# A hybrid decoder layer in float32: another order for the first loads, a shorter run-up and a shared first cast

## The chip, the cores and the metric

The kernel runs on one core of a Trainium2 chip. The metric is the device time of one execution in microseconds. A core has TensorE (PE in the profile, its weight loads PEld), VectorE (DVE), ScalarE (ACT), GpSimd (POOL) and SyncE (SP); DMAs are issued here by SyncE and ScalarE, each on a queue of its own.

## The reference, cut to what matters

One decoder layer over a sequence of 256 tokens with 2048 channels, all in float32. The change touches only the way into the first projection:

```python
h = rmsnorm(x, norm_mix_w[l])                       # x: (1, 256, 2048)
proj = jnp.einsum('bsd,de->bse', h, w_in[l])        # 2048 -> 14368 columns
q, k, v, z, b_raw, a_raw, p_in, g_a, g_b = jnp.split(proj, splits, axis=-1)
...                                                 # gated delta rule, pooling mixer, gates
x = x + jnp.einsum('bsd,de->bse', mixed, w_out[l])
...                                                 # norm, up projection, convolution, GELU
x = x + jnp.einsum('bsf,fd->bsd', jax.nn.gelu(gate, approximate=False) * up, w_down[l])
return rmsnorm(x, norm_final_w)
```

The per-token scale of the norm commutes with the product, so the kernel multiplies x only by the norm's channel weights before the projection and applies the scale later.

## The kernel before

Every large product is done in two parts per operand. A float32 tile is split into an upper part (a cast to fp32r, on ScalarE) and the rest (a subtraction on VectorE), and three products are added in PSUM: upper x times upper weight, lower x times upper weight, upper x times lower weight. Weights come as a list `srcs` of tiles of 256 rows by 512 columns (512 KB each). `load(n)` issues DMAs on SyncE until n tiles have been asked for, into four buffers `raw`; the first two tiles (`HALVES`) go as two DMAs of 256 KB each. `begin(n)` splits tiles into `whi` (L144, ScalarE) and `wlo` (L152, VectorE); for the first two tiles `begin_half(n, k)` does one half of 128 rows (L133, L134).

The start is written out by hand, and PE, DVE and ACT run it in the order of the program:

- `ones` and `ident` are made on GpSimd, and `runup(9)` lets TensorE multiply `ones` by `ones` nine times (L243). Each of these float32 products is two matmul records in the trace.
- ScalarE's queue loads `nmrows`, the norm's channel weights as 16 rows (L255). ScalarE then does one small copy, `first` (L258), ahead of which its function table is loaded.
- SyncE's queue loads x in four blocks of 512 columns, `x0[0]` to `x0[3]` (L263), with the weight tiles in between. The first block goes as two DMAs of 256 columns. The order is: x first half, weight tile 0 (two DMAs), x second half, weight tile 1 (two DMAs), x block 1, tiles 2 and 3, x blocks 2 and 3.
- TensorE transposes `nmrows` (L321) and VectorE copies the result to `nmw`, one weight for each partition and block of 128 channels.
- `turn_x` transposes x (L281), `parts_x` makes from each transposed block the upper part `xhi` on ScalarE (L287) and the lower part `xlo` on VectorE (L288), both scaled by `nmw`, and `products_k0` runs the products (L313): four with `whi`, then two with `wlo`, for each 128 channels.
- In the first round of the loop over halves there are no products yet; `runup(4)` is there in their place.

Then three blocks of x follow in the same way, and after them the rest of the layer, with weights loaded, split and multiplied in a steady order.

Of the kernel before, what the change touches and what calls it, by code (L numbers as in the profile page):

```python
# [7 lines left out]
F32 = mybir.dt.float32  # L8
# [5 lines left out]
P = 128  # L14
# [20 lines left out]
def kernel(  # L35
# [20 lines left out]
    nc = tc.nc  # L56
# [11 lines left out]
    def nm(s):  # L68
        cnt[0] += 1
        return f"{s}_{cnt[0]}"  # L70

    def pg(shape=(P, 512)):
        return psg.tile(list(shape), F32, tag="g", name=nm("psg"))
# [35 lines left out]
    loads = []  # L109
# [4 lines left out]
    def weights(ahead=AHEAD):  # L114

        begin(taken[0] + ahead + 1)
        taken[0] += 1
        return made[taken[0] - 1]

    def load(n):  # L120
        while len(loads) < min(len(srcs), n):
            src = srcs[len(loads)]
            raw = wpool.tile(list(src.shape), F32, tag="raw", name=nm("raw"), bufs=4)
            for k in range(2) if len(loads) < HALVES else (slice(None),):
                last_load[0] = nc.sync.dma_start(raw[:, k], src[:, k]).ins
            loads.append(raw)

    def begin_half(n, k):

        if k == 0:  # L130
            made.append(tuple(wpool.tile([P, 2, 512], F32R, tag=tag, name=nm(tag)) for tag in ("whi", "wlo")))
        hi, lo = made[n]
        nc.scalar.copy(hi[:, k], loads[n][:, k])  # L133
        nc.vector.tensor_tensor(lo[:, k], loads[n][:, k], hi[:, k].bitcast(F32), op=ALU.subtract)  # L134

    def begin(n):
        while len(made) < min(len(srcs), n):
            load(len(made) + 1)
            raw = loads[len(made)]
            shape = list(raw.shape)  # L140
            keep = kept.get(len(made))
            hi = wpool.tile(shape, F32R, tag="whi", name=nm("whi")) if keep is None else \
                mtile(keep, shape, F32R, nm("khi"))
            nc.scalar.copy(hi, raw)  # L144
            if shape[1] == 8:
                lo = None
                nc.vector.tensor_tensor(hi[:, :, 32:64], raw[:, :, 0:32], hi[:, :, 0:32].bitcast(F32),
                                        op=ALU.subtract)
            else:
                lo = wpool.tile(shape, F32R, tag="wlo", name=nm("wlo")) if keep is None else \  # L150
                    mtile(4 + keep, shape, F32R, nm("klo"))
                last_split[0] = nc.vector.tensor_tensor(lo, raw, hi.bitcast(F32), op=ALU.subtract).ins  # L152
            made.append((hi, lo))
# [87 lines left out]
    def runup(n):  # L241
        for _ in range(n):
            mm(pr0[:, 0, :P], ones, ones, start=True, stop=True)  # L243


    runup(9)

    def mtile(i, shape, dt, name):
        return big.tile(shape, dt, tag=f"m{i}", name=name)

    mix = tc.tile_pool(name="mix", bufs=1)
    mp = mix.__enter__()

    nmrows = mp.tile([KD, P], F32, tag="w1", name="nmrows")
    rows = nc.scalar.dma_start(nmrows, norm_mix_w[0].rearrange("(r p) -> r p", p=P))  # L255
    first = cpool.tile([P, 1], F32, name="first")
    with tc.issue_after(rows.ins):
        nc.scalar.copy(first, ones[:, 0:1])  # L258
    x0 = []
    for c in range(4):  # L260
        xc = mtile(c, [P, 2, 512], F32, f"x0_{c}")
        for h in ((0, 256), (256, 512)) if c == 0 else ((0, 512),):
            nc.sync.dma_start(xc[:, :, h[0] : h[1]], x[0, :, c * 512 + h[0] : c * 512 + h[1]]  # L263
                              .rearrange("(t p) d -> p t d", p=P))
            if h[0] == 0:
                load(min(c + 1, 4))
        x0.append(xc)
        load(min(2 * c + 2, 4))


    nmw = cpool.tile([P, KD], F32, name="nmw")
# [3 lines left out]
    def turn_x(c, ks=range(4)):  # L275

        pts = []
        for k in (4 * c + k for k in ks):
            pt = pg([P, S])
            for t in range(2):  # L280
                nc.tensor.transpose(pt[:, t * P : (t + 1) * P], x0[c][:, t, (k % 4) * P : (k % 4 + 1) * P], ident)  # L281
            pts.append((k, pt))
        return pts

    def parts_x(pts):
        for k, pt in pts:
            hi = nc.scalar.activation(xhi[:, k, :], pt, AF.Copy, scale=nmw[:, k : k + 1])  # L287
            lo = nc.vector.scalar_tensor_tensor(xlo[:, k, :], pt, nmw[:, k : k + 1], xhi[:, k, :].bitcast(F32),  # L288
                                                op0=ALU.mult, op1=ALU.subtract)
        return hi.ins, lo.ins  # L290
# [3 lines left out]
    def square_x(c):  # L294
        for t in range(2):
            junk = cpool.tile([P, 512], F32, tag="sqj", name=nm("junk"))
            nc.scalar.activation(junk, x0[c][:, t, :], AF.Square, accum_out=ssq4[:, t, c : c + 1])
# [10 lines left out]
    def products_k0(c, kks, hi, lo):  # L308
        for w, part in ((hi, xh), (hi, xl), (lo, xh)):
            for kk in kks:  # L310
                k = 2 * c + kk
                for t in range(2):
                    mm(ps_k0[:, t, :], part(k, t), w[:, kk, :], start=(k == 0 and w is hi and part is xh),  # L313
                       stop=(k == KD - 1 and w is lo))

    def tile_k0(c):
        products_k0(c, range(2), *weights(-1))

    with tc.manual_schedule(engines={mybir.EngineType.PE, mybir.EngineType.DVE, mybir.EngineType.Activation}):
        pt = pg()  # L320
        nc.tensor.transpose(pt[:, :KD], nmrows, ident[:KD, :KD])  # L321
        nc.vector.tensor_copy(nmw, pt[:, :KD])

        n = 0
        for c in range(HALVES):
            for k in range(2):
                if k == 0:
                    pts = turn_x(0, (2 * c, 2 * c + 1))
                parts_x(pts[k : k + 1])
                begin_half(c, k)  # L330
                if n == 0:
                    runup(4)
                else:
                    products_k0((n - 1) // 2, ((n - 1) % 2,), *made[(n - 1) // 2])
                n += 1
        taken[0] = HALVES
        for c in range(4):
            if c:
                tile_k0(2 * c)
            if c < 3:  # L340
                pts = turn_x(c + 1)
                parts_x(pts[:2])
                begin(2 * c + 3)
                last_act, last_dve = parts_x(pts[2:])
                begin(2 * c + 4)
                square_x(c)
            if c:
                tile_k0(2 * c + 1)
            else:
                products_k0(1, (1,), *made[1])  # L350
        square_x(3)
# [110 lines left out]
    for c in range(2):  # L462
        hi, lo = weights()
        for kk in range(8):
            k = 8 * c + kk
# [556 lines left out]
    for c in range(4):  # L1022
# [9 lines left out]
        for k2 in range(2):  # L1032
            pt = pg([P, 2, S])
            for kk in range(2):
                k = 4 * c + 2 * k2 + kk
                for t in range(2):
                    nc.tensor.transpose(pt[:, kk, t * P : (t + 1) * P], xt[:, t, k * P : (k + 1) * P], ident)
            for kk in range(2):
                k = 4 * c + 2 * k2 + kk
# [76 lines left out]
    for t in range(2):  # L1116
# [31 lines left out]
        n = len(blocks) - 1  # L1148
# [39 lines left out]
```

## Time and profile before

| | us |
|---|---|
| median of three runs | 1562.16 (1561.58 to 1562.27) |
| the profiled execution, its own time | 1561.54 |
| its span, first to last instruction | 1559.8 |
| TensorE busy | 1551.1 (99%) |
| VectorE busy | 1092.2 (70%) |
| ScalarE busy | 749.2 (48%) |
| DMA, mean over the span | 195 GB/s |

The profile is one execution of the program. A line in the timeline gives the start and the duration in microseconds, the engine, the line of the kernel, the operation and what it writes and reads. The names are those of the program without buffer numbers: `xhl` is the tile that holds `xhi` and `xlo`, `x` is `x0`. An `SPq` or `ACTq` line is the issue of a DMA, not the transfer; the DMA view gives the time from issue to landing.

### The profile page before, as it was taken

Reading aid. Unit: us, or ns where it says so; the run is one execution under the profiler, and the core shown is the slowest. Engines: PE = TensorE matmul, PEld = TensorE weight load, DVE = VectorE, ACT = ScalarE, POOL = GpSimd, SP = SyncE. Lnnn points to the kernel's source line nnn. Section 1 sums busy time; section 2 is a strip of 40 time slices with the busy share of each in tenths; the row PEclk is TensorE's granted clock in tenths of the full one; section 3 lists DMA queues with packets and bytes.
Section 4 is the critical chain, followed back from the end, with each engine's and each line's share of the span. In section 5 each row is a group of like instructions: output and inputs, shape, how many; then the busy total and the mean of one; then the engine's idle time right before and its main releaser. Section 6 shows DMA issues by size and latency. Waiting matters only on the chain.

```text
span 1559.8 us, 21250 instructions
## 1 busy us (share of the span) xinstructions
PE 1551.1 (99%) x7996; PEld 1304.0 (84%) x7996; DVE 1092.2 (70%) x1705; ACT 749.2 (48%) x969; POOL 52.2 (3%) x54
## 2 busy tenths in 40 slices
PE   9999999999999999999999999999999999999998
PEld 8878888888888888888888888888888888888886
DVE  6899758996699858896656666776666667444445
ACT  6545445454555445454544544444444444334443
POOL 1020001000010001000000000000000000000000
PEclk9999999999999999999999999999999999999999
DMA  8677657676676656675666666666666666666662
GB/s 273 201 239 200 186 161 223 204 204 183 174 218 202 194 174 191 211 205 174 216 188 176 190 188 189 189 190 188 189 183 195 188 187 212 196 192 210 200 222 93
DMA packets 168229, 304.21 MB, mean 195 GB/s; under 512 B 19235, under 2 KB 22835, under 8 KB 167999
## 3 DMA queue, kind: packets, MB, share of 16 engines
q1 hardware_dynamic: 165104, 297.84, 64.5%
q10 hardware_dynamic: 3022, 5.03, 1.0%
q8 instruction: 62, 1.02, 0.3%
q14 instruction: 41, 0.33, 0.1%
HBM read 297.56 MB, written 5.27 MB: 194 GB/s over the span
## 4 chain that ended last, share of the span: by engine, by line
PE 99%; issue 1%; ACT 0%; DVE 0%; POOL 0%; POOLq 0%
PE psm L182 15%; PE psm L184 15%; PE psm L183 15%; PE psm L206 11%; PE psg L206 10%; PE psg L1094 8%; PE psm L1094 7%; PE psg L207 5%; PE psm L207 5%; PE psm L313 1%; PE psg L672 1%; PE psg L227 1%; PE psg L674 0%; PE psm L243 0%; PE psg L809 0%
## 5 line engine op out<-in xcount | busy, mean ns | idle before, releaser
L152 DVE TENSOR_TENSOR wlo<-raw,whi 128x1024 fp32r<-128x1024 f32 x522 | 636.8, 1222 | 376.6 <-ACT whi L144 372.0
L144 ACT CAST whi<-raw 128x1024 fp32r<-128x1024 f32 x524 | 551.3, 1053 | 699.5 <-PE psm L183 293.8
L184 PE MATMUL psm<-wlo,xhl 128*128 128x512 f32 x864 | 339.1, 393 | 0.0
L183 PE MATMUL psm<-whi,xhl 128*128 128x512 f32 x864 | 339.0, 392 | 0.0
L182 PE MATMUL psm<-whi,xhl 128*128 128x512 f32 x864 | 339.0, 392 | 0.0
L206 PE MATMUL psm<-fhl,whi 128*128 128x512 f32 x704 | 246.2, 396 | 0.0
L206 PE MATMUL psg<-fhl,whi 128*128 128x512 f32 x704 | 238.0, 394 | 0.0
L207 PE MATMUL psm<-fhl,wlo 128*128 128x256 f32 x704 | 194.4, 279 | 0.0
L182 PEld LDWEIGHTS psm<-whi,xhl 128*128 128x128 f32 x864 | 162.3, 188 | 33.0
L183 PEld LDWEIGHTS psm<-whi,xhl 128*128 128x128 f32 x864 | 162.3, 188 | 32.9
L184 PEld LDWEIGHTS psm<-wlo,xhl 128*128 128x128 f32 x864 | 162.2, 188 | 32.7
L207 PE MATMUL psg<-fhl,wlo 128*128 128x256 f32 x704 | 178.7, 279 | 0.0
L206 PEld LDWEIGHTS psm<-fhl,whi 128*128 128x128 f32 x704 | 131.4, 188 | 30.5
L206 PEld LDWEIGHTS psg<-fhl,whi 128*128 128x128 f32 x704 | 129.2, 188 | 24.1
L207 PEld LDWEIGHTS psg<-fhl,wlo 128*128 128x128 f32 x704 | 132.5, 188 | 6.9
L207 PEld LDWEIGHTS psm<-fhl,wlo 128*128 128x128 f32 x704 | 132.6, 188 | 1.1
L1094 PE MATMUL psg<-whi,hhi 128*128 128x512 f32 (+1 forms) x170 | 66.0, 389 | 0.0
L1094 PE MATMUL psg<-whi,hlo 128*128 128x512 f32 (+1 forms) x170 | 65.9, 388 | 0.0
L1094 PE MATMUL psm<-whi,hlo 128*128 128x512 f32 x168 | 65.1, 388 | 0.0
L1094 PE MATMUL psm<-wlo,hhi 128*128 128x512 f32 x168 | 65.1, 388 | 0.0
L1094 PE MATMUL psm<-whi,hhi 128*128 128x512 f32 x168 | 65.1, 388 | 0.0
L1094 PE MATMUL psg<-wlo,hhi 128*128 128x512 f32 (+1 forms) x170 | 59.6, 388 | 0.0
(280 smaller groups left out, 1533.9 us busy)
## 6 DMA issues: line engine op xcount, KB each, us to landing
raw<-in_w_in_dram SPq DMA_DIRECT2D x224, 512.0 KB, 4.3
raw<-in_w_up_dram SPq DMA_DIRECT2D x176, 512.0 KB, 4.4
raw<-in_w_down_dram SPq DMA_DIRECT2D x88, 512.0 KB, 4.3
raw<-in_w_out_dram SPq DMA_DIRECT2D x32, 512.0 KB, 3.8
mv<-vrow SPq DMA_DIRECT2D x12, 512.0 KB, 5.7
taps<-in_conv_qkv_w_dram SPq DMA_DIRECT2D x16, 256.0 KB, 6.0
raw<-in_pool_w_dram SPq DMA_DIRECT2D x8, 512.0 KB, 3.7
vrow<-ev SPq DMA_DIRECT2D x4, 512.0 KB, 4.1
```

The costliest lines, as they stand in the source:

```text
L144: nc.scalar.copy(hi, raw)
L152: last_split[0] = nc.vector.tensor_tensor(lo, raw, hi.bitcast(F32), op=ALU.subtract).ins
L182: mm(ps[:, t, :], lh(k, t), hi[:, kk, :], start=(k == 0), stop=False)
L183: mm(ps[:, t, :], ll(k, t), hi[:, kk, :], start=False, stop=False)
L184: mm(ps[:, t, :], lh(k, t), lo[:, kk, :], start=False, stop=(k == nk - 1))
L206: mm(ps[f], hi[:, kk, fs], rhl(k), start=(k == 0), stop=False, skip_group_check=True)
L207: mm(ps[f][:, 1, :], lo[:, kk, fs], rhl(k)[:, 0, :], start=False, stop=(k == nk - 1), skip_group_check=True)
L227: nc.tensor.transpose(pt[:, ff, t * P : (t + 1) * P], src[:, t, f * P : (f + 1) * P], ident)
L313: mm(ps_k0[:, t, :], part(k, t), w[:, kk, :], start=(k == 0 and w is hi and part is xh), stop=(k == KD - 1 and w is lo))
L672: mm(pg0, kq[:, h, 0, 0:P], kq[:, h, :, :], start=True, stop=True)
L1094: mm(ps[:, cs], part(k, t), w[:, kk, cs], start=(k == first and n == 0), stop=(k == KF - 1 and n == 2), skip_group_check=last_block)
```

## The change

- `x0` is allocated ahead of the loads, and a helper `load_x(queue, c, h)` issues a part of it.
- The first half of the first x block is issued on ScalarE's queue, ahead of `nmrows`. SyncE's queue begins with weight tile 0; the order of the rest is as it was.
- `runup(9)` becomes `runup(7)`, and `runup(4)` in the first round is dropped.
- In `begin_half`, the very first half tile (n = 0, k = 0) is cast by two engines: columns 0 to 255 by ScalarE, columns 256 to 511 by VectorE. The other halves are cast by ScalarE alone.

```diff
     def begin_half(n, k):
...
-        nc.scalar.copy(hi[:, k], loads[n][:, k])
+        if n or k:
+            nc.scalar.copy(hi[:, k], loads[n][:, k])
+        else:
+            nc.scalar.copy(hi[:, k, :256], loads[n][:, k, :256])
+            nc.vector.tensor_copy(hi[:, k, 256:], loads[n][:, k, 256:])
         nc.vector.tensor_tensor(lo[:, k], loads[n][:, k], hi[:, k].bitcast(F32), op=ALU.subtract)
...
-    runup(9)
+    runup(7)
...
+    x0 = [mtile(c, [P, 2, 512], F32, f"x0_{c}") for c in range(4)]
+
+    def load_x(queue, c, h):
+        queue.dma_start(x0[c][:, :, h[0] : h[1]], x[0, :, c * 512 + h[0] : c * 512 + h[1]]
+                        .rearrange("(t p) d -> p t d", p=P))
+
+    load_x(nc.scalar, 0, (0, 256))
     nmrows = mp.tile([KD, P], F32, tag="w1", name="nmrows")
     rows = nc.scalar.dma_start(nmrows, norm_mix_w[0].rearrange("(r p) -> r p", p=P))
     first = cpool.tile([P, 1], F32, name="first")
     with tc.issue_after(rows.ins):
         nc.scalar.copy(first, ones[:, 0:1])
-    x0 = []
-    for c in range(4):
-        xc = mtile(c, [P, 2, 512], F32, f"x0_{c}")
-        for h in ((0, 256), (256, 512)) if c == 0 else ((0, 512),):
-            nc.sync.dma_start(xc[:, :, h[0] : h[1]], x[0, :, c * 512 + h[0] : c * 512 + h[1]]
-                              .rearrange("(t p) d -> p t d", p=P))
-            if h[0] == 0:
-                load(min(c + 1, 4))
-        x0.append(xc)
-        load(min(2 * c + 2, 4))
+    for n, c, h in ((1, 0, (256, 512)), (2, 1, (0, 512)), (4, 2, (0, 512)), (4, 3, (0, 512))):
+        load(n)
+        load_x(nc.sync, c, h)
...
                 begin_half(c, k)
-                if n == 0:
-                    runup(4)
-                else:
+                if n:
                     products_k0((n - 1) // 2, ((n - 1) % 2,), *made[(n - 1) // 2])
                 n += 1
```

## The prediction

> **What bounds the kernel now.** I read the head of the page first, then the waits of TensorE, then the stretch in which the program starts.
>
> ```profile
> span 1559.8 us, 21250 instructions
> PE 1551.1 (99%) x7996; PEld 1304.0 (84%) x7996; DVE 1092.2 (70%) x1705; ACT 749.2 (48%) x969; POOL 52.2 (3%) x54
> PE 99%; issue 1%; ACT 0%; DVE 0%; POOL 0%; POOLq 0%
> PE psm L243 <- POOL ones L233: 1.1, 1, 1.1
> 6.86:20.00 13.14, 13.14 (x68) 10.90 (x68) 9.86 (x16) 10.44 (x22) 0.00 (x0) 1.00 1.04 378
> ```
>
> The chain that ended last is TensorE for 99% of the span, and the only wait that the waits view lists for TensorE in the whole run is the 1.1 us for the first memset. The last row (a window; the columns are its length, the busy time and count of PE, PEld, DVE, ACT, POOL, then the granted clock, the DMA share and GB/s) says that this holds in the first microseconds as well: from 6.86 us on, TensorE has no idle time. So what comes before the first product is a constant in front of 1553 us of TensorE work, and whatever moves that product moves the end by as much, as long as nothing behind it starts to wait. The change touches only what lies before that product, and the instructions of all engines behind it stand in the same order as before.
>
> The start itself, from the timeline (start us, duration us, engine, line):
>
> ```profile
> 0.80 0.45 ACTq L255 DMA_DIRECT2D nmrows<-in_norm_mix_w_dram  x1
> 0.81 0.43 SPq L263 DMA_DIRECT2D x<-in_x_dram  x1
> 1.06 4.21 PE L243 MATMUL psm<-ones 128*128 128x128 f32 x18 [1.06 <-POOL ones L233]
> 1.28 0.93 SPq L125 DMA_DIRECT2D raw<-in_w_in_dram  x2
> 1.29 1.28 ACT L258 ACT_TABLE_LOAD   x1 [1.29 <-PEq L1172]
> 2.59 0.19 ACT L258 COPY first<-ones 128x1 f32<-128x1 f32 x1
> 5.20 0.23 PE L321 MATMUL psg<-ident,nmrows 16*128 16x16 f32 x1
> 5.36 0.66 PE L281 MATMUL psg<-ident,x 128*128 128x128 f32 x4
> 5.83 0.47 ACT L287 ACTIVATE xhl<-psg,nmw 128x256 fp32r<-128x256 f32 x1 [3.05 <-PE psg L281]
> 5.85 1.06 PE L243 MATMUL psm<-ones 128*128 128x128 f32 x8
> 6.21 0.61 ACT L133 CAST whi<-raw 128x512 fp32r<-128x512 f32 x1
> 6.34 0.48 DVE L288 SCALAR_TENSOR_TENSOR xhl<-psg,nmw,xhl 128x256 fp32r<-128x256 f32 x1 [0.70 <-ACT xhl L287]
> 6.71 0.48 ACT L287 ACTIVATE xhl<-psg,nmw 128x256 fp32r<-128x256 f32 x1
> 6.85 0.69 DVE L134 TENSOR_TENSOR wlo<-raw,whi 128x512 fp32r<-128x512 f32 x1
> 6.87 1.20 PE L313 MATMUL psm<-whi,xhl 128*128 128x512 f32 x4
> ```
>
> Nine run-up products are 18 passes and hold TensorE until 5.20. The norm row's transpose (L321) and those of x follow, ScalarE makes the upper part of x at 5.83, is free for its next instruction 0.38 later, casts the weights from 6.21 to 6.82, and the first product starts 0.05 later, at 6.87. The transfers, from the DMA view of narrow windows (KB each, us from issue to landing):
>
> ```profile
> x<-in_x_dram SPq DMA_DIRECT2D x1, 256.0 KB, 3.2
> raw<-in_w_in_dram SPq DMA_DIRECT2D x1, 256.0 KB, 4.9
> q10 hardware_dynamic: 32, 0.01, 1.1%
> 1.06:5.20 4.14, 4.14 (x19) 3.92 (x19) 2.54 (x11) 1.48 (x2) 2.65 (x9) 1.00 0.61 147
> ```
>
> The first block of x, issued at 0.81, lands at about 4.05; the first weights, issued at 1.28, at about 6.2; ScalarE's queue (q10; the row is of the window from 0 to 3.3 us, and the windows after it up to 12 us have none of it) has moved the norm row by 3.3. So two things set the first product today: the run-up keeps TensorE from x, which has been there for 1.1 us, and the weights land just when ScalarE is free for them.
>
> **The change part by part.**
>
> *Run-up of 7 in place of 9.* Four passes go. 18 passes took 4.21 us with the last one's tail; from the first start at 1.06 to the next work at 5.20 they held TensorE 4.14, or 0.23 each, so it is free 0.92 earlier: 4.28. The other run-up of four (8 passes from 5.85) goes too. It would end near 6.9 with its tail, in the shadow of the cast that ends at 6.82; it costs nothing today and saves nothing, unless the first product could start before about 6.8.
>
> *x on ScalarE's queue, the norm row behind it.* x is issued at the same time as before (0.80 against 0.81). The norm row is issued 0.45 later. It is transposed ahead of x on TensorE, so it now counts: it has to come after x on the same queue. If x keeps its landing of 4.05 and the row follows by its own issue time, it lands at 4.5, and L321 starts at 4.6 with 0.1 for the signal. Lower bound: both are there when TensorE is free, 4.28. Upper bound: the weights, which SyncE now issues at the same moment, take every second packet; 147 GB/s moved in that window, so the 256 KB that get in between cost 1.8 us, and L321 starts at 5.9. I take 4.6, near the lower end, because the DMA engines were busy only 0.61 of that window. What is queued behind the two issues on ScalarE moves 0.48 later: the table load and the copy, which end at 2.78 now and would at 3.26; ScalarE's next work is after 5. Hidden by over 1.5 us.
>
> *First weights issued first on SyncE.* Issue at 0.81 in place of 1.28, so landing near 5.7 at the same 4.9; the second half of x and the later weights also move up one place of 0.47 on SyncE.
>
> *First cast shared.* ScalarE casts 256 of 512 columns, VectorE the others. VectorE is in order, and its cast stands behind the lower part of x (0.48 at L288) and ahead of wlo. Today the chain from the start of ScalarE's x (5.83) is 0.38 + 0.61 + 0.05 = 1.04 to the first product. Shared, it is 0.51 until VectorE starts its part of x (6.34 less 5.83), 0.51 until it is free (6.85 less 6.34), the cast, and 0.05. The trace has no such cast; the rows on both sides of it:
>
> ```profile
> L733 DVE COPY tb<-idb 128x256 f32<-128x256 f32 x4 | 1.1, 288 | 0.0
> L410 DVE COPY rb<-psg 128x256 f32<-128x256 f32 x1 | 0.4, 417 | 0.0
> L430 DVE CAST lowr<-low 128x128 fp32r<-128x128 f32 x1 | 0.4, 361 | 0.0
> ```
>
> The same width takes 0.29 between buffers and 0.42 from PSUM. I take 0.35, between them, because the one cast to fp32r needs 0.36 for half the width, beside a busy GpSimd. So the chain is 1.42, 0.38 longer than today's: the sharing pays only where the weights land after VectorE could have been done with x. ScalarE's own half lies beside this. The cast also puts wlo behind it: today wlo starts 0.02 before the first product, then as well, and TensorE asks for it only after four products; that wait stays as far off as it is.
>
> *The sum.* L321 at 4.60; ScalarE's x 0.63 later (5.83 less 5.20) at 5.23; the first product 1.42 later at 6.65. VectorE reaches the cast at 6.25, the weights are there at 5.7, so they do not bind. 6.65 against 6.87 is 0.22 earlier. With L321 at 4.28 and a cast of 0.29 it would be 6.27 (0.6 earlier); with 5.9 and 0.42, 8.02 (1.15 later).
>
> *What is late next.* The transfers behind have room:
>
> ```profile
> raw<-in_w_in_dram SPq DMA_DIRECT2D x1, 512.0 KB, 8.0
> 12.70 1.05 ACT L144 CAST whi<-raw 128x1024 fp32r<-128x1024 f32 x1
> 14.37 1.07 ACT L144 CAST whi<-raw 128x1024 fp32r<-128x1024 f32 x1
> ```
>
> The first row is the fourth weight tile, issued at 5.22: it lands at 13.2 and is cast at 14.37, 1.1 later. A gain of 0.2 to 0.6 fits into that, so it is kept to the end.
>
> The profiled run took 1561.54, 1.74 more than its span, so the sum gives 1561.3. The median of the runs shown is 0.62 above that run (1562.16), and the difference of 0.22 stands against it: 1561.9. A difference of 0.2%, 3.1 us, is about what a measurement of this kernel can tell from no change; this one is far below.
>
> **One rule of the Trainium skill on the queues.** The page "DMA: Bandwidth & Descriptors", section "Issuing engines are not separate DMA queues", says that transfers from several engines run on the same 16 DMA engines, interleaved, and that a second issuer saves only issue time. By it, moving x brings at most the 0.47 of one issue, for the weights, and what x loses to them is rival C below; the 0.61 row neither confirms nor denies it.
>
> **The rivals.**
>
> *A: earlier still.* x and the norm row are there when TensorE is free: 0.6 earlier, 1561.6. For it: x landed at 4.05. Against: the row must come behind x. Chance 0.13.
>
> *B: slower, the clock stays at half.* 18 run-up passes took 4.21, but the 8 after 5.85 took 1.06: 0.23 against 0.13 each. The doubling came somewhere between the start at 1.06 and 5.36, after at most 4.3 us of unbroken work; the passes up to the end of the run-up show no speed-up, so not much sooner. The new run-up is 3.2 us, then come a pause of 0.3, 0.5 of transposes and a pause of over 1 us. If that does not count as enough, products run at half speed until up to 4.3 us after they begin, which loses half of it: 2.1 us, 1564.1. Against it:
>
> ```profile
> 1552.20:1554.85 2.65, 0.00 (x0) 0.00 (x0) 1.41 (x6) 1.15 (x4) 0.56 (x1) 1.00 0.00 0
> 1554.86:1559.80 4.94, 0.00 (x0) 0.00 (x0) 0.49 (x1) 0.68 (x2) 0.00 (x0) 0.50 0.57 212
> ```
>
> At the end TensorE is idle for 2.65 us before the granted clock falls from 1.00 to 0.50: a clock once granted survives pauses longer than the new ones. It decides whether the grant comes with the shorter run-up. Chance 0.2. The Trainium skill, "TensorE: Matmul & The Clock Gate", Part 1, has the grant come after one busy window of about 3.4 us that runs free of the kernel's start; by that, a run of 3.2 us may or may not fill one, and a miss would cost an estimated 1.7. The trace's at most 4.3 us agrees with such a window and does not show how full it must be.
>
> *C: slower, x late behind the weights.* The upper end above: L321 at 5.9, the first product 1.15 later, 1563.3. It decides from L321 later than 4.8, where the longer cast chain eats the rest. Against: the engines had spare time. Chance 0.08.
>
> *D: the change does nothing*, because the weights land no earlier than today and bind at 6.2: with the halves side by side the product comes near 6.65 to 6.9 all the same. 1562.1, chance 0.04, and the same time as the forecast to what can be told.
>
> **How the numbers follow.** The forecast, 0.2 earlier, has 0.55; A 0.13, B 0.2, C 0.08, D 0.04. The three runs shown are spread over 0.7 (1561.58 to 1562.27), which goes on both ends: low is A less 0.6, 1561.0; high is B, 1564.1, which also holds C. Faster by over 3.1 us would need a first product before 3.8, when the run-up still runs: 0.02 for what I have not seen. Slower by over 3.1 needs B and C together (1562.16 plus 2.1 and 1.15) or a grant that is missed twice: 0.05. The rest, 0.93, is the same.
>
> **What would show it.** Right: L321 between 4.4 and 4.8, VectorE's cast of 0.3 to 0.4 ending just before the first L313 at 6.5 to 6.8, 0.11 between passes of the transposes, and no idle TensorE after it. Wrong: products 0.43 apart or more after the start (B); L321 after 4.8 (C); a first product before 6.4 (A); or TensorE waiting between 7 and 20 us for x or weights that landed later than before.

## The result: 0.29% slower, and the profile after

The changed kernel takes 1566.57 us (median of 8 runs, 1565.69 to 1566.92) against 1562.04 (8 runs, 1561.32 to 1563.05): a ratio of 1.0029, 95% interval 1.0019 to 1.0039. That is 4.5 us, more than the top of the range (1564.1). The profiled run took 1566.41 with a span of 1564.7, 4.9 longer than before. From the page of the changed kernel, its waits views for TensorE and SyncE, and its timeline:

```profile
span 1564.7 us, 21228 instructions
PE 1552.3 (99%) x7984; PEld 1303.8 (83%) x7984; DVE 1092.1 (70%) x1706; ACT 748.6 (48%) x969; POOL 52.2 (3%) x54
PE psg L326 <- DMA nmrows<-in_norm_mix_w_dram: 2.6, 1, 2.6
PE psm L318 <- DVE whi L137: 1.1, 1, 1.1
SPq L125 <- DMA x<-in_x_dram: 2.0, 1, 2.0
0.80 0.47 ACTq L262 DMA_DIRECT2D x<-in_x_dram  x1
0.80 0.85 SPq L125 DMA_DIRECT2D raw<-in_w_in_dram  x2
1.06 3.22 PE L247 MATMUL psm<-ones 128*128 128x128 f32 x14 [1.06 <-POOL ones L237]
1.31 0.48 ACTq L267 DMA_DIRECT2D nmrows<-in_norm_mix_w_dram  x1
5.81 0.89 SPq L125 DMA_DIRECT2D raw<-in_w_in_dram  x2
6.84 0.20 PE L326 MATMUL psg<-ident,nmrows 16*128 16x16 f32 x1 [2.56 <-DMA nmrows<-in_norm_mix_w_dram]
6.97 0.73 PE L286 MATMUL psg<-ident,x 128*128 128x128 f32 x4
7.45 0.47 ACT L292 ACTIVATE xhl<-psg,nmw 128x256 fp32r<-128x256 f32 x1 [4.14 <-PE psg L286]
7.82 0.40 ACT L136 CAST whi<-raw 128x256 fp32r<-128x256 f32 x1
7.95 0.48 DVE L293 SCALAR_TENSOR_TENSOR xhl<-psg,nmw,xhl 128x256 fp32r<-128x256 f32 x1 [0.70 <-ACT xhl L292]
8.36 0.28 DVE L137 CAST whi<-raw 128x256 fp32r<-128x256 f32 x1
8.78 2.05 PE L318 MATMUL psm<-whi,xhl 128*128 128x512 f32 x4 [1.08 <-DVE whi L137]
18.25 2.10 PE L318 MATMUL psm<-whi,xhl 128*128 128x512 f32 x8
```

TensorE had one wait before; it has two more now. The shortened run-up ends at 4.28, as forecast. Then TensorE stands until 6.84: the norm row has not landed. x is late as well: SyncE's issue at 5.81 is one that waits for the landing of x, which came at 4.05 before. The first product starts at 8.78, 1.91 later than before. And the first four products take 2.05 where they took 1.20. The stretches of the same trace (length, busy time and count of the five engines, granted clock, DMA share, GB/s) say why:

```profile
0.60:4.00 3.40, 2.94 (x14) 2.94 (x14) 2.63 (x11) 1.47 (x2) 2.88 (x11) 1.00 0.55 86
4.01:7.41 3.40, 0.84 (x7) 0.63 (x6) 0.17 (x1) 0.00 (x0) 0.00 (x0) 1.00 1.03 337
7.42:10.82 3.40, 2.32 (x7) 1.68 (x6) 2.37 (x5) 1.65 (x4) 0.00 (x0) 0.50 1.05 389
10.84:14.24 3.40, 3.40 (x11) 2.71 (x11) 1.56 (x4) 1.86 (x4) 0.00 (x0) 0.50 1.05 388
14.25:20.00 5.75, 5.75 (x30) 4.63 (x30) 3.26 (x6) 3.60 (x7) 0.00 (x0) 1.00 0.62 202
```

The clock was at full speed after the run-up (the transposes of x, 0.73 for four, are those of a full clock), was lost after 3.4 us in which TensorE worked 0.84, stayed at half through a stretch with 2.32 of work and one of unbroken work, and came back at 14.24. The 1.00 of the first row says nothing: its 14 passes took 3.22, or 0.23 each, against 0.13 at full speed before, and the trace's record of the clock only begins with the first grant, at 4.00 here. This is the course of one execution. The mean granted clock is 0.996 in three of the eight runs, this one among them, and 0.998 in the five others at much the same times; how the clock went in those five is not known. The last row of the timeline above, the eight products of the third weight tile, stood at 13.82 before: 4.43 later now. Of that, 1.91 is the late first product and 2.5 the half clock. The spans differ by another 0.4, which arises near 490 us and is spoken of below.

Did the second queue bring more bytes? The same two stretches, first before, then after:

```profile
1.80:3.30 1.50, 1.50 (x9) 1.50 (x8) 1.50 (x6) 0.97 (x2) 1.40 (x4) 1.00 0.85 203
3.30:5.20 1.90, 1.90 (x11) 1.68 (x9) 0.30 (x2) 0.00 (x0) 0.53 (x2) 1.00 0.65 160
```

```profile
1.80:3.30 1.50, 1.50 (x9) 1.50 (x8) 1.50 (x6) 1.47 (x2) 1.40 (x4) 1.00 0.96 126
3.30:5.20 1.90, 0.98 (x6) 0.78 (x4) 0.29 (x2) 0.01 (x1) 0.52 (x2) 1.00 0.84 203
```

No: over the 3.4 us it is (203 × 1.5 + 160 × 1.9) / 3.4 = 179 GB/s before and 169 after, while the stretches from 4 to 14 us move 337 to 389. The idle share of the DMA engines was not room for a second queue. x only shared what there was with the weights, and not evenly. The DMA view of the changed kernel from 0 to 5.80 us, when x has landed, has for SyncE's queue (q1) and ScalarE's (q10; packets, MB, share of the engines):

```profile
q1 hardware_dynamic: 302, 0.53, 41.2%
q10 hardware_dynamic: 285, 0.27, 21.5%
```

While x was on its way, SyncE's queue moved twice the bytes of x. Its packets are larger, 1.8 KB against 0.9 in the mean, and it began sooner: up to 2.8 us the view has its packets alone (0.12 MB).

### The profile page after: what moved, and what is told of

It reads as the page before. It is cut to its first block, busy times and chain, and to the rows that moved or that the text cites. A ratio compares the mean times of both kernels' runs of the same rounds, so it can differ in the third digit from the quotient of the medians.

```text
span 1564.7 us, 21228 instructions
## 1 busy us (share of the span) xinstructions
PE 1552.3 (99%) x7984; PEld 1303.8 (83%) x7984; DVE 1092.1 (70%) x1706; ACT 748.6 (48%) x969; POOL 52.2 (3%) x54
## 3 DMA queue, kind: packets, MB, share of 16 engines
q8 instruction: 62, 1.02, 0.3%
## 4 chain that ended last, share of the span: by engine, by line
PE 98%; issue 1%; DMA 0%; ACT 0%; DVE 0%; POOLq 0%; POOL 0%; ACTq 0%
PE psm L188 15%; PE psm L186 15%; PE psm L187 15%; PE psm L210 10%; PE psg L210 10%; PE psg L1097 7%; PE psm L1097 7%; PE psg L211 5%; PE psm L211 5%; PE psm L318 2%; PE psg L675 1%; PE psg L231 1%; PE psg L677 0%; DMA nmrows<-in_norm_mix_w_dram 0%; PE psg L820 0%
```

## The experiments

Two theories stood against each other. ORDER: x and the norm row land late because the weights are issued beside them, and the half clock follows from the pause that this makes behind a short run-up. RUN-UP: the short run-up loses the clock by itself. Times are medians of 10 or 11 runs, and ratios are to the kernel before on the same chip.

### The loads alone: q_only

```diff
 the changed kernel, with
-    runup(7)
+    runup(9)
+                if n == 0: runup(4)      # as before
+        nc.scalar.copy(hi[:, k], loads[n][:, k])   # cast by ScalarE alone
```

> Before, with the order of the loads changed alone (x first half on ScalarE's queue ahead of the norm row, SyncE starting with the weights); run-up of 9 and of 4 kept, first cast by ScalarE alone. Theory ORDER (x and the norm row land late because the weights are issued beside them, and the pause this makes costs the clock only where the run-up is short): norm row's transpose at 6.8 us, first product at 6.8 + 1.67 = 8.5, clock at full speed from then on, 1562.0 + 1.6 = 1563.6. Theory RUN-UP (the short run-up by itself loses the clock, whatever the loads do): the same 1563.6. If the pause costs the clock even after the long run-up: about 1566.

1564.74 us, ratio 1.0017 (1.0008 to 1.0026). From its timeline:

```profile
6.84 0.26 PE L322 MATMUL psg<-ident,nmrows 16*128 16x16 f32 x1 [1.57 <-DMA nmrows<-in_norm_mix_w_dram]
7.03 1.12 PE L282 MATMUL psg<-ident,x 128*128 128x128 f32 x4
7.93 1.91 PE L243 MATMUL psm<-ones 128*128 128x128 f32 x8
9.50 1.52 PE L314 MATMUL psm<-whi,xhl 128*128 128x512 f32 x4
```

The order of the loads alone makes the kernel slower, and the row comes at 6.84 as in the changed kernel. My 1563.6 was too low, and the 1566 of the other case too high: four transposes of x take 1.12 in place of 0.66 and the eight run-up passes 1.91 in place of 1.06, so the clock was at half here too, and the passes hold the first product to 9.50. It was not lost in the pause: the trace's record of the clock begins with a grant at 10.28, so in this execution even the run-up of nine, 4.2 us without a break, had brought none.

### The run-up alone: r_only, and with the second one kept: r_fill

```diff
 the kernel before, with
-    runup(9)
+    runup(7)
-                if n == 0: runup(4)      # r_only; r_fill keeps this line
```

> Before, with the run-up of 7 in place of 9 and without the second one alone. ORDER: norm row's transpose at 4.3, weights still land at 6.2 and bind, first product at 6.87 as before, full clock, 1562.0. RUN-UP: the pause from about 4.9 to 6.87 behind a short run-up drops or delays the grant, products 0.43 apart at first, 1562.0 + 2.5 = 1564.5.

> Before, with the first run-up of 7 in place of 9 alone; the second one stays. The clock theory (a window of work with few gaps) has the second run-up close the gap that r_only left open: first product at 6.6 to 6.9, full clock in nearly every run, median 1562.0. If the length of the first run-up decides: runs of 1563 to 1564 as in r_only, whose median was 1563.5.

r_only: 1563.49 us (1561.66 to 1564.06), ratio 1.0006 (0.9996 to 1.0015). r_fill: 1561.92 (1561.29 to 1563.21), 0.9999 (0.9990 to 1.0008). r_only's timeline:

```profile
4.34 0.28 PE L321 MATMUL psg<-ident,nmrows 16*128 16x16 f32 x1
6.59 2.08 PE L313 MATMUL psm<-whi,xhl 128*128 128x512 f32 x4 [0.92 <-ACT whi L133]
9.76 1.19 PE L313 MATMUL psm<-whi,xhl 128*128 128x512 f32 x4
```

So RUN-UP is partly right. The row is transposed at 4.34 and the first product is even 0.3 earlier than in the trace of before, but four products take 2.08 until the clock comes, at 9.48 by the trace's record. The median is 1.4 above before, which the interval does not quite tell from nothing. With the second run-up back, r_fill is at the time of before: its first grant is at 7.02, behind a stretch without a break, and six of the ten runs of r_only are above all eleven of r_fill. So the work that the prediction dropped as lying "in the shadow of the cast" brought the clock sooner. Not all of the 1.6 between the medians is the clock: at 480 us the two traces are 0.9 apart, and 0.8 more arise near 490 us (see below).

### The shared cast alone: s_only

```diff
 the kernel before, with
-        nc.scalar.copy(hi[:, k], loads[n][:, k])
+        if n or k: ...                   # as in the change
```

> Before, with the first cast shared by ScalarE and VectorE alone. By the prediction's chain VectorE's half stands behind its part of x: first product at 6.85 + 0.28 + 0.05 = 7.18, 0.3 later, 1562.3. Rival: the halves run side by side from the landing at 6.2 and the product comes at 6.65, 0.2 earlier, 1561.8.

1562.15 us, ratio 1.0001 (0.9991 to 1.0010). From its timeline:

```profile
5.41 0.93 PE L285 MATMUL psg<-ident,x 128*128 128x128 f32 x4
6.64 0.48 DVE L292 SCALAR_TENSOR_TENSOR xhl<-psg,nmw,xhl 128x256 fp32r<-128x256 f32 x1 [0.95 <-ACT xhl L291]
7.04 0.28 DVE L137 CAST whi<-raw 128x256 fp32r<-128x256 f32 x1
7.47 1.17 PE L317 MATMUL psm<-whi,xhl 128*128 128x512 f32 x4 [0.24 <-ACT xhl L291]
```

VectorE's half does stand behind its part of x, as the prediction had it, and takes 0.28. The product is 0.3 later still than expected: the transposes of x, at 0.93 in place of 0.66, ran in part at half clock in this execution, and VectorE reaches its part of x at 6.64 in place of 6.34. In time the sharing is nothing that can be told.

### The loads put back: q_undone, and with the second run-up: q_fill

```diff
 the changed kernel, with the loads of before; q_fill also has
+                if n == 0: runup(4)
```

> The changed kernel with the loads in the order of before (x first on SyncE, norm row alone on ScalarE's queue); run-up of 7, no second one, shared cast. ORDER: norm row's transpose at 4.3, both halves of the cast from the landing at 6.2, first product at 6.6, full clock, 1561.8. RUN-UP: first product at 6.6 but at half clock for some 5 us, 1564.3.

> The changed kernel with the loads in the order of before and the second run-up of 4 put back (run-up of 7, shared cast). First product at 6.7 with the clock full in every run: median 1561.9, against 1562.7 of q_undone, whose runs went up to 1564.0. If the second run-up does nothing for the clock: 1562.7 again.

q_undone: 1562.66 us (1561.70 to 1563.97), ratio 1.0003 (0.9994 to 1.0012). q_fill: 1561.45 (1561.22 to 1562.59), 0.9996 (0.9988 to 1.0005). With the loads put back, 3.9 of the 4.5 us are gone. q_undone's trace has the full clock and the first product at 6.69, but its runs spread over 2.3 us; with the second run-up they spread over 1.4, and the median is 1.2 lower. The two traces do not put this down to the clock: q_undone is 0.1 ahead of q_fill at 480 us and ends 0.8 behind it, and all of that arises near 490 us. Against the kernel before no gain can be told.

### TensorE kept busy through the wait: long_run

```diff
 the changed kernel, with
-    runup(7)
+    runup(16)
+                if n == 0: runup(6)
```

> The changed kernel with run-ups of 16 and 6 in place of 7 and none, so that TensorE works through the wait for the norm row. If the clock's half speed is the second part of the loss: the clock is granted once before 7.3 us and stays, first product at 8.8 as in the changed kernel, so 1562.1 + 1.9 = 1564.0 (with up to 0.9 more from the stretch near 500 us, where runs differ). If the late product alone explains the loss: 1566.5, as before.

1564.00 us, ratio 1.0011 (1.0002 to 1.0021). The loads are those of the changed kernel:

```profile
7.53 0.23 PE L326 MATMUL psg<-ident,nmrows 16*128 16x16 f32 x1
8.18 1.50 PE L247 MATMUL psm<-ones 128*128 128x128 f32 x12
9.51 1.17 PE L318 MATMUL psm<-whi,xhl 128*128 128x512 f32 x4
16.41 2.11 PE L318 MATMUL psm<-whi,xhl 128*128 128x512 f32 x8
```

The first product is later still, at 9.51, since this run-up is longer than the wait; but the four products take 1.17, and 2.6 us of the loss are gone. The third weight tile is at 16.41, 1.84 ahead of the changed kernel, although the first product is 0.73 behind it: that makes 2.57 for the half clock, which is shown to be that part. That the median is just the 1564.0 expected is luck, since the expectation had the product at 8.8.

### The norm row ahead of x: row_first

```diff
 the changed kernel, with
-    load_x(nc.scalar, 0, (0, 256))
     rows = nc.scalar.dma_start(nmrows, ...)
+    load_x(nc.scalar, 0, (0, 256))
```

> The changed kernel with the norm row ahead of the first half of x on ScalarE's queue. If the row's place behind x costs what the landings say (5.8 for x, 6.7 for the row): the row's transpose comes at 4.3, those of x at about 6.2, first product near 8.1 in place of 8.8, the half clock stays, 1565.9. If what lands second on that queue is simply late, whichever it is: transposes of x at 6.8 or later, 1566.5.

1565.74 us, ratio 1.0023 (1.0013 to 1.0033). Timeline, then the stretches of the clock:

```profile
6.38 0.66 PE L286 MATMUL psg<-ident,x 128*128 128x128 f32 x4 [1.65 <-DMA x<-in_x_dram]
8.19 2.05 PE L318 MATMUL psm<-whi,xhl 128*128 128x512 f32 x4 [1.16 <-DVE whi L137]
4.21:7.61 3.40, 1.02 (x6) 0.55 (x5) 0.42 (x2) 0.76 (x3) 0.00 (x0) 1.00 1.04 366
7.62:11.02 3.40, 2.83 (x7) 2.17 (x8) 2.11 (x5) 0.88 (x2) 0.00 (x0) 0.50 1.05 390
11.03:20.00 8.97, 8.97 (x50) 7.43 (x49) 6.19 (x10) 6.97 (x15) 0.00 (x0) 1.00 0.83 280
```

TensorE now waits for x itself, which lands at 6.3, and the product comes 0.6 sooner than in the changed kernel, although x is issued 0.45 later and lands 0.5 later here. So the row's place behind x cost at least 0.6 of the 1.9, and by the landings in the changed kernel (x at 5.80, the row at 6.70) up to 0.9; the rest is x's lateness, which this run does not set apart.

### x with its head start back: x_alone

```diff
 the changed kernel, with
-    rows = nc.scalar.dma_start(nmrows, ...)
+    rows = nc.sync.dma_start(nmrows, ...)    # ahead of the weights on SyncE
-    with tc.issue_after(rows.ins):           # the copy `first` has no place behind the row now
```

> The changed kernel with the norm row moved to the head of SyncE's queue, so that the first weights are issued at 1.3 as before, behind the x block that ScalarE's queue issues at 0.8. TIME: x has its head start back and lands at 4.1, first product at 6.7, 1562 (to 1563 by the clock's luck). RING: the weights take turns with x, x lands at 5 or later, first product at 7.5 or later, 1563.5 or more; the same holds if ScalarE's queue starts slower than SyncE's for a block of 256 pieces.

1561.99 us, ratio 1.0000 (0.9990 to 1.0009). x is still on ScalarE's queue beside the weights, but these are now issued 0.45 after it:

```profile
4.56 0.66 PE L285 MATMUL psg<-ident,x 128*128 128x128 f32 x4
6.47 1.21 PE L317 MATMUL psm<-whi,xhl 128*128 128x512 f32 x4 [1.25 <-ACT whi L136]
4.51:7.91 3.40, 2.15 (x11) 1.62 (x12) 2.40 (x6) 1.76 (x4) 0.00 (x0) 1.00 0.96 358
7.92:20.00 12.08, 12.08 (x64) 9.96 (x63) 8.76 (x15) 9.95 (x20) 0.00 (x0) 1.00 1.04 380
```

x is there without a wait at 4.56 (it landed at 3.8), and the first product is 0.4 ahead of before. ScalarE's queue is not slow for such a block; the half microsecond of head start was what counted, since the row, which left this queue, had stood behind x. The time is no better than before: in this trace the 0.3 that is left of the lead at 480 us turns into 0.5 behind near 490 us.

### The first weights on ScalarE's queue: w_on_act

```diff
 the changed kernel, with x first on SyncE's queue, and in load():
-                last_load[0] = nc.sync.dma_start(...)
+                last_load[0] = (nc.scalar if len(loads) == 0 and k == 0 else nc.sync).dma_start(...)
```

> The changed kernel with x first on SyncE's queue (issue at 0.8) and the first half weight tile on ScalarE's queue behind the norm row (issue at 1.3): the issue times of before, but weights and x on different queues. TIME (what is issued first is served first): x lands at 4.05 as before, the weights at 6 or a little sooner, first product at 6.6, 1562 (to 1563, by the clock's luck with the short run-up). RING (two queues take turns, so a second queue takes bandwidth from x even when it is issued later): x lands at 4.5 or later, its transposes after that, first product at 7 or later, 1563 or more.

1564.14 us, ratio 1.0009 (1.0000 to 1.0019). x was on time; the weights were not (timeline):

```profile
6.88 0.29 DVE L137 CAST whi<-raw 128x256 fp32r<-128x256 f32 x1 [1.11 <-DMA raw<-in_w_in_dram]
7.34 2.08 PE L319 MATMUL psm<-whi,xhl 128*128 128x512 f32 x4 [2.38 <-ACT whi L136]
```

Neither expectation holds whole: TIME is right for x, but the first weights, issued together with others on SyncE, land at 6.9, 0.7 later than the same issue time gave before; the clock is at half again (2.08 for four products). Here the one on the second queue was the late one.

### A faster version? x_fill and x_fill_plain

```diff
 x_alone, with
+                if n == 0: runup(4)
 x_fill_plain: also the first cast by ScalarE alone
```

> x_alone (x first on ScalarE's queue, norm row first on SyncE's, weights behind it, shared cast, run-up of 7) with the second run-up of 4 put back. TIME, and the clock needing nearly unbroken work: first product at 6.5, 0.4 ahead of before, the clock at full speed by then in every run; median 1561.7, less scatter than x_alone (its slowest run was 1564.8), and no run above 1563.5. If the second run-up does nothing for the clock: as x_alone, with single runs of 1564 and more.

> x_fill with the first cast by ScalarE alone. In this order the weights land after VectorE is free, so the shared cast should help here: without it the first product comes at 6.0 + 0.61 + 0.05 = 6.67 in place of 6.47, median 0.2 above x_fill. If the sharing costs here as well, the product comes at 6.4 or sooner.

x_fill: 1562.11 us (1561.07 to 1563.10), ratio 1.0000 (0.9991 to 1.0009). x_fill_plain: 1561.67 (1561.20 to 1563.02), 1.0000 (0.9991 to 1.0008). The scatter is smaller than x_alone's, as expected, but only by the one run of x_alone at 1564.78 (the other nine end at 1562.40), and there is no gain, and the sharing does not show the 0.2 that I gave it. In x_fill's profiled run the clock came late and the second run-up itself held the first product:

```profile
5.46 1.77 PE L247 MATMUL psm<-ones 128*128 128x128 f32 x8
6.99 1.17 PE L317 MATMUL psm<-whi,xhl 128*128 128x512 f32 x4
```

So none of the twelve beats the kernel before by more than can be told.

## Why the prediction was wrong, step by step

- **What bounds the kernel: right in the main.** The late first product and the slow products after it were carried to the end: 4.43 at the third tile, 4.5 in the medians. But that nothing behind the start begins to wait did not hold near 490 us (below).
- **Run-up of 7 frees TensorE at 4.28: right**, and worth nothing, since nothing was there to do.
- **L321 at 4.60: this step failed.** It came at 6.84, beyond my upper bound of 5.9. I kept x at its landing of 4.05 and let the row follow by its issue time, because the DMA engines were busy for only 0.61 of the window; that share was not room. With the weights issued at the same moment x landed at 5.80. The upper end had this (1.8 lost from 4.05), but by luck: 0.53 MB of other loads went past x, against 0.12 MB before, so 0.41 MB more and not 256 KB, and faster than the 147 GB/s of the sum. It also let the row follow x at once, and the row landed 0.9 behind it, at 6.70. Rival C was the mechanism and had 0.08.
- **The rule of the Trainium skill on the queues was right.** "DMA: Bandwidth & Descriptors", "Issuing engines are not separate DMA queues", has transfers of several engines interleave on the same DMA engines; the 179 against 169 GB/s agree. What I put above it, one busy share, was worse.
- **The second run-up saves and costs nothing: wrong.** As work it lies in a shadow, but it fills the gap that the clock looks at (r_only against r_fill, 1563.5 against 1561.9, of which about half comes from the start by their traces).
- **"A clock once granted survives pauses longer than the new ones": wrong.** The row at the end of the kernel showed an idle stretch of 2.65 up to the fall, not how long a pause is safe. Here the pause was 2.56, shorter than that, and the clock went: 0.84 of work in 3.4 us lost it, and in row_first so did 1.02; 2.15 in x_alone kept it.
- **Rival B's price of 2.1: near**, 2.5 measured, but not by B's way: in this trace the short run-up did bring the grant, at 4.00, and the pause lost it. I made B and C separate cases, with 0.05 for both together. They are one case: a late x makes the pause that loses the clock. Even their sum, 3.25, is short of the 4.4 measured, by 0.8 at the first product and 0.4 at the clock.
- **The cast chain: the size right, the step harmless.** VectorE's cast took 0.28 against 0.35. From ScalarE's x at 7.45 to the product are 1.33 against 1.42.

The last 0.4 of the span's difference goes with a wait of VectorE near 490 us for `lb`, a load that is no part of the change. Its row in the waits of VectorE from 484 to 495 us, before and in q_undone:

```profile
DVE tmp L736 <- DMA lb<-cdd: 0.7, 1, 0.7
DVE tmp L738 <- DMA lb<-cdd: 3.0, 1, 3.0
```

Laid beside the trace of before, the other thirteen traces are later at 530 us than at 480 us by 0 to 0.9. Where this wait is 0.4 to 2.0 that growth is nothing; where it is 2.5 to 3.0 it is 0.4 to 0.9, each time the wait less some 2.2. The changed kernel waits 2.6. The six traces with a growth are those without the second run-up; the seven others have one, of 4 or 6. With one trace for each kernel this is an observation, and why the load is later there stays open. So part of what the second run-up seems to save is not the clock.

## What to carry to other kernels

Here a second queue for the first loads added no bandwidth, at a start that moves half of what it moves later: it took from what was needed first. Issue the transfer that heads the chain alone and half a microsecond ahead, and put nothing that the chain needs behind a large one on its queue. Before dropping idle-time work on TensorE, ask what the granted clock does in the gap it leaves, and treat a late input and a lost clock as one event.

## What the runs showed of the hardware

- The clock is decided in steps of 3.41 us: in the changed kernel the half-speed stretch is 7.42 to 14.24, two steps, in row_first 7.62 to 11.03, one. "TensorE: Matmul & The Clock Gate", Part 1, in the Trainium skill gives such a free-running window; the steps agree with it. A step with 2.32 us of work did not bring the clock back, one with 2.94 granted it (the rows of the changed kernel), and 2.15 was enough to keep it (x_alone). The busy column gives no clean limit: in r_only the step from 2.66 to 6.07, with 3.01, brought no grant, and the next, with 2.88, did.
- The steps do not start with the kernel: their edges lay at other times in the traces (7.42, 7.62, 4.51), and a run-up of 4.2 us ended in a grant at 5.20 before and in none in q_only. So a start with gaps is a matter of luck from run to run, which is where much of the 2.3 us of spread in q_undone and the 2.4 in r_only would come from. That it does was not tried by itself.
- The DMA engines moved 126 to 203 GB/s in the stretches from 1.8 to 5.2 us (before and changed), and 337 to 390 in the stretches of 3.4 us behind 4 us (changed, row_first, x_alone), with one queue or two. Why the start is slow stays open.
